# Order of the block products and of the transposes in the first MLP matrices of a two-layer decoder trunk

## The chip, the cores and the metric

The kernel runs on one core of a Trainium2 chip. Its time is the device time of one execution in microseconds. Five engines take part, each with its own queue that is worked off in order: TensorE (PE, with its weight loads PEld), VectorE (DVE), ScalarE (ACT), GpSimd (POOL) and SyncE (SP). SP and POOL only start DMAs here. Engines wait for each other through semaphores.

## The reference

Two decoder layers over 256 tokens of width 2048 in float32. Layer 0 mixes by two recurrent groups, layer 1 by dilated attention; behind each mixer stands an MLP with 8192 hidden features, and a norm closes the whole:

```
def squared_relu_mlp(h, w1, w2):
    return jnp.square(jax.nn.relu(h @ w1)) @ w2

for layer in range(DEPTH):
    hn = rms_norm(h, norm_mix[layer])
    ...
    h = h + mix
    h = h + squared_relu_mlp(rms_norm(h, norm_mlp[layer]), mlp_w1[layer], mlp_w2[layer])
return rms_norm(h, final_norm)
```

The change touches the products with `w1` and, in a detail, with `w2`.

## The kernel before, in words

**Weights.** All weights come from memory in units of 128 partitions x 2048 float32, 1 MB each, in a fixed list (`units`). A unit is loaded by SP into a `raw` tile (three buffers), and then split into two parts: ScalarE copies it into `hi` (line 102), VectorE subtracts and leaves `lo` (line 103); both have three buffers, too. So a unit's split can start once the unit three places before it has been multiplied, and its load once the raw tile three places before it has been split. A product in full precision takes three matmuls for each block of 128 features: x-high with `hi`, x-high with `lo`, x-low with `hi`, in this order (`times`). `unit()` hands out the next unit and fetches ahead, about three units.

**The MLP.** `mlp` goes through the hidden features in four quarters of 2048. For each quarter, `first` is called twice (for `w1`, n = 0 and 2, each gives 1024 of the quarter's features) and then `second` twice (for `w2`, each adds to 1024 of the output columns). Each of these four calls is one run of `blocks`: eight 1 MB blocks of weights, and 180 matmuls of 512 columns. Half of the contraction is done by a scheme of the Strassen kind, with seven block products of 12 matmuls instead of eight; the other half is plain.

The seven products and their operands, by name: a and d multiply plain weight blocks (units 0 and 1); t1, t2, t3 and t4 multiply sums of weight blocks, c multiplies block 5. VectorE makes the sums at line 130: s = a + t1 when a is fetched, s += c when the unit ahead of t2 is fetched. Two sums are made by DMAs that POOL starts and that add in place: t1 += block 5 (line 142, at the same fetch), and, for `w1` alone, s += block 1 (line 148, at the fetch of c), which t4 needs. `t1` and `s` have one buffer each. The plain half consists of four units called n (n6, n7, n2, n3), each with 24 matmuls: 12 for each half of the tokens.

**The banks.** `blocks` holds four accumulators: alpha, delta and gamma of one pool, beta of another that alternates between two banks from block to block. a, t2, t3 and t4 go to beta, t1 and c to alpha, d to gamma. n6 and n7 add to delta and then alpha, n2 and n3 to gamma and then beta. Between products the results that are needed by themselves are read out: in `first`, after a, t1 and t2 by a ScalarE copy (`hold`, line 716), after t3 by VectorE (`u3`, lines 729 and 730), after the last plain product of a sum by `final` (line 742). ScalarE then applies the squared ReLU (lines 720 and 721).

**The transposes.** What a block leaves is put in a list `later` as a function: `to_h` (eight transposes on TensorE, then copies at lines 696 and 697 and the forms for the next matrices at lines 593 to 600) after `first`, and `to_features` (transposes, then lines 235 and 236) after a projection and, in layer 0's last quarter, after `second`. `flush` runs what was in the list at a given moment. In `blocks`, `due` is taken before each n, and the flush stands after its 24 matmuls.

**What sets the order.** TensorE's matmuls and transposes are chained in the order of the program (`mm`, `turn`). The other engines' queues are ordered when the program is built, by a scheduler with priorities (`stream` and `urgent`). The order of the units within a block is written out by hand at the end of the file: `ORDERS[0]` for `w1`, `ORDERS[1]` for `w2`. `plan2` uses it for the list of units, `blocks` for the products.

```
_A = (("a", 0), ("t1", 4))
_B = (("t2", 5), ("c", None))
_C = (("t3", None), ("d", 1), ("n", 2), ("t4", None), ("n", 3))
ORDERS = (_A + (("n", 6),) + _B + (("n", 7),) + _C, _A + (("n", 7),) + _B + (("n", 6),) + _C)
```

Of the kernel before, what the change touches and what calls it, by code (L numbers as in the profile page):

```python
# [41 lines left out]
def trunk_kernel(ctx, tc, x, xtok, cols, tab, masks, pos, fin, w_in, w_gate, w_out, w_qkv, w_o, w1, w2, out):  # L42
# [28 lines left out]
    def plan2(src, i):  # L71
        for what, u in ORDERS[src is w2]:
            units.append((src, None if u is None else i + u, what, i))
# [3 lines left out]
    for step in ORDER.split():  # L77
        src, first, n = where[step[0]]
# [29 lines left out]
    def fetch():  # L108
        u = at[0]
        if u >= len(units):  # L110
            return
        at[0] += 1
        src, i = units[u][:2]
        with stream():
            if len(units[u]) > 2:
                combine(u, *units[u])
                return
            r = wraw.tile([P, 2048], F32, name="raw")
            nc.sync.dma_start(r, src[i])
            made[u] = Weights(r, 1024)  # L120
# [49 lines left out]
    def unit(src, i):  # L170
        u = at[1]
        assert units[u][0] is src and units[u][1] in (None, i), (u, i)
        at[1] += 1
        if u + 2 >= at[0]:
            fetch()
        return made.pop(u)
# [3 lines left out]
    def mm(*args, **kw):  # L180
        chain[:] = [after(T.matmul(*args, **kw), chain)]  # L181
# [4 lines left out]
    later = []  # L186

    def flush(due=None):
        todo = later[:due]
        del later[:due]  # L190
        for f in todo:
            f()
# [455 lines left out]
    def blocks(src, i0, n0, mov, forms, events, final):  # L648
        plain = lambda j, k: (mov[:, k, j * P:j * P + P], mov[:, k, S + j * P:S + j * P + P])
        form = lambda f, k: (forms[:, k, 0, f * P:f * P + P], forms[:, k, 1, f * P:f * P + P])  # L650
        side = {"a": lambda i: plain(0, 2 * i), "d": lambda i: plain(0, 2 * i + 1), "t4": lambda i: plain(1, 2 * i + 1),
                "t1": lambda i: form(3, i), "t2": lambda i: form(0, i), "t3": lambda i: form(1, i),
                "c": lambda i: form(2, i)}
        alpha, delta, gamma = (pmm.tile([P, 512], F32, name="p") for _ in range(3))
        beta = psc.tile([P, 512], F32, name="po" if n0 else "pd", bufs=1)
        bank = {"a": beta, "t1": alpha, "t2": beta, "c": alpha, "t3": beta, "d": gamma, "t4": beta}
        sums = {(0, 0): gamma, (0, 1): beta, (1, 0): alpha, (1, 1): delta}
        opened = []

        def times(bank, w, get):  # L660
            for i in range(4):
                h, l = w.part(i * 512, 512)
                xh, xl = get(i)
                mm(bank, xh, h, start=not any(b is bank for b in opened), stop=False, skip_group_check=True)
                opened.append(bank)
                mm(bank, xh, l, start=False, stop=False, skip_group_check=True)
                mm(bank, xl, h, start=False, stop=i == 3, skip_group_check=True)

        plains = [0, 0]
        for what, u in ORDERS[src is w2]:  # L670
            w = unit(src, None if u is None else i0 + 4 * n0 + u)
            if what != "n":
                times(bank[what], w, side[what])
                if what in events:
                    events[what](bank[what])
                continue
            n, g = divmod(u, 4)
            plains[n] += 1
            due = len(later)
            for j in (1, 0) if n else (0, 1):  # L680
                times(sums[n, j], w, lambda i, j=j, g=g: plain(j, 4 * g + i))
                if plains[n] == 2:
                    final(n, j, sums[n, j])
            flush(due)
# [24 lines left out]
    def first(i0, n0):  # L709
# [23 lines left out]
        def final(n, j, bank):  # L733
            with urgent():
# [5 lines left out]
                else:  # L740
                    y = keep["y2" if n else "y1"]
                    V.tensor_tensor(y, bank, y, OP.subtract if n else OP.add)
                    relu2(n, j, y, y)

        blocks(w1, i0, n0, bufa, formx, {"a": hold("y1", 2), "t1": hold("y4"), "t2": hold("y2"), "t3": u3}, final)

    def second(i0, n0, nrm, r2, r2n, done, gains):
        def to_x(bank, j, n, r, last):
            at = slice(n * 512, n * 512 + 512)
            with urgent():  # L750
                V.scalar_tensor_tensor(xres[:, j, at], bank, r[:, j:j + 1], xres[:, j, at], op0=OP.mult, op1=OP.add)  # L751
                if nrm and last:
                    nrm.add(j, n)

        def u2(bank):
            to_x(bank, 0, n0 + 1, r2n, False)
            if gains:
                gains()

        def u3(bank):  # L760
            to_x(bank, 1, n0 + 1, r2n, True)
            done(n0 + 1)

        blocks(w2, i0, n0, bufb, formh,
               {"a": lambda b: to_x(b, 0, n0, r2, False), "t1": lambda b: to_x(b, 1, n0 + 1, r2, False),
                "t2": u2, "t3": u3},
               lambda n, j, b: to_x(b, j, n0 + n, r2, (n, j) != (1, 1)))
        done(n0)
# [186 lines left out]
WARM = 12  # L955
LINE = 64
SCRATCH = 4096
_A = (("a", 0), ("t1", 4))
_B = (("t2", 5), ("c", None))
_C = (("t3", None), ("d", 1), ("n", 2), ("t4", None), ("n", 3))  # L960
ORDERS = (_A + (("n", 6),) + _B + (("n", 7),) + _C, _A + (("n", 7),) + _B + (("n", 6),) + _C)
T4_DMA = lambda w1, w2: (w1,)
NOSYNC = mybir.DependencyInfo(mybir.DependencyClass.NoSync, mybir.DependencyReason.DATA)

# [102 lines left out]
```

## Time and profile before

| what | us |
|---|---|
| median of 3 runs | 2178.93 (2178.92 to 2179.68) |
| the profiled execution | 2178.8 |
| its span, first to last instruction | 2177.0 |
| TensorE busy | 2148.7 |
| VectorE busy | 1783.6 |
| ScalarE busy | 1261.1 |

The page gives busy time and waits over one execution; lines are those of the kernel before. The two MLPs run from about 426 to 1107 us and from about 1490 us to the end. In the timeline a row gives start, duration, engine, line, operation, output and inputs, and in brackets the idle time before it with what ended it. A row that begins with SPq or POOL is a DMA's start on that queue, not its transfer; the view of the DMA issues gives the time from issue to landing. Matmuls overlap: each is shown with 0.39 us, and they follow each other at a shorter distance, which is read from their starts.

```profile
DMA  8444445577777677787655554556768777777873
...
q1 hardware_dynamic: 58176, 410.89, 53.2%
q0 software_dynamic: 7264, 51.42, 12.8%
...
L103 DVE TENSOR_TENSOR lo<-raw,hi 128x1024 fp32r<-128x1024 f32 (+2 forms) x486 | 822.3, 1709 | 237.7 <-ACT hi L102 219.3
```

The first row is the mean busy share of the 16 DMA engines in 40 slices, in tenths. q1 holds the loads that SP starts, q0 the adding loads that POOL starts, each with its packets, MB and share of the DMA engines' time. The last row is the group of VectorE's splits.

### The profile page before, as it was taken

To read this page: it belongs to the slowest core of one execution; us is meant where nothing else is said; L and a number is where in the kernel's file an instruction comes from. 1 tells how busy PE (TensorE), PEld (TensorE's weight loads), DVE (VectorE), ACT (ScalarE), POOL (GpSimd) and SP (SyncE) were. 2 spreads that over 40 slices of the span, in tenths; PEclk is the share of its full clock that TensorE was granted. 3 is DMA by queue.
4 is the path that set the end of the run, shared out by engine and by line. 5 is a ranking of instruction groups with operands and counts; after the bars stand their busy time and mean duration, and the time that the engine had idled before them with its cause. 6 is when DMAs were issued, how large, how long until landed. Compare 5 with 4: busy or idle time off the path is not lost.

```text
span 2177.0 us, 27718 instructions
## 1 busy us (share of the span) xinstructions
PE 2148.7 (99%) x11044; PEld 1834.7 (84%) x11044; DVE 1783.6 (82%) x2078; ACT 1261.1 (58%) x1429; POOL 44.6 (2%) x57
## 2 busy tenths in 40 slices
PE   9999999999999999999999999999999999999997
PEld 8999998878888888888788888888888888888886
DVE  7776787779879889888877778667898898898897
ACT  7444485566466566466554544455655755755664
POOL 0000000000000000000000000000000000000000
PEclk9999999999999999999999999999999999999999
DMA  8444445577777677787655554556768777777873
GB/s 317 155 157 170 149 156 207 189 235 240 228 236 248 226 247 232 232 251 231 201 207 169 179 175 163 185 193 213 232 221 258 237 224 238 251 231 224 260 238 129
DMA packets 65857, 464.68 MB, mean 213 GB/s; under 512 B 7344, under 2 KB 8112, under 8 KB 10304
## 3 DMA queue, kind: packets, MB, share of 16 engines
q1 hardware_dynamic: 58176, 410.89, 53.2%
q0 software_dynamic: 7264, 51.42, 12.8%
q8 instruction: 87, 1.43, 0.3%
q10 hardware_dynamic: 288, 0.61, 0.1%
q14 instruction: 42, 0.34, 0.0%
HBM read 460.78 MB, written 2.10 MB: 213 GB/s over the span
## 4 chain that ended last, share of the span: by engine, by line
PE 89%; ACT 5%; DVE 3%; issue 2%; DMA 1%; SPq 0%; DVEq 0%; ACTq 0%
PE p L181 63%; PE po L181 11%; PE pd L181 10%; ACT hi L102 3%; PE pl L184 2%; DVE lo L103 1%; PE pl L476 1%; DMA raw<-in_w 0%; ACT y L720 0%; ACT formh L593 0%; ACT y L716 0%; ACT y L721 0%; PE pl L864 0%; DMA xall<-in_x 0%; PE po L885 0%
## 5 line engine op out<-in xcount | busy, mean ns | idle before, releaser
L102 ACT CAST hi<-raw 128x1024 fp32r<-128x1024 f32 (+2 forms) x486 | 689.2, 1443 | 571.4 <-PE p L181 403.1
L103 DVE TENSOR_TENSOR lo<-raw,hi 128x1024 fp32r<-128x1024 f32 (+2 forms) x486 | 822.3, 1709 | 237.7 <-ACT hi L102 219.3
L181 PE MATMUL p<-hi,bufb 128*128 128x512 f32 x1408 | 448.5, 390 | 2.2 <-DVE xall L751 2.1
L181 PE MATMUL p<-hi,bufa 128*128 128x512 f32 x1280 | 412.5, 392 | 11.3 <-ACT y L716 7.9
L181 PE MATMUL p<-bufa,hi 128*128 128x256 f32 (+1 forms) x1792 | 364.9, 317 | 0.1
L181 PEld LDWEIGHTS p<-hi,bufb 128*128 128x128 f32 x1408 | 264.3, 188 | 60.0 <-DVE xall L751 5.6
L181 PEld LDWEIGHTS p<-bufa,hi 128*128 128x128 f32 x1792 | 294.5, 190 | 18.9 <-DVE hz L418 0.3
L181 PEld LDWEIGHTS p<-hi,bufa 128*128 128x128 f32 x1280 | 240.4, 188 | 65.5 <-ACT y L716 11.3
L181 PE MATMUL p<-lo,bufb 128*128 128x512 f32 x704 | 274.1, 389 | 1.0 <-DVE lo L103 1.0
L181 PE MATMUL p<-bufa,lo 128*128 128x256 f32 x1152 | 255.5, 287 | 0.0
L181 PE MATMUL p<-lo,bufa 128*128 128x512 f32 x640 | 250.5, 391 | 1.9 <-DVE lo L103 1.9
L103 DVE TENSOR_TENSOR lo<-s,hi 128x2048 fp32r<-128x2048 f32 x96 | 219.5, 2287 | 23.2 <-ACT hi L102 21.3
L102 ACT CAST hi<-s 128x2048 fp32r<-128x2048 f32 x96 | 183.7, 1913 | 48.1 <-PE po L181 21.7
L181 PEld LDWEIGHTS p<-bufa,lo 128*128 128x128 f32 x1152 | 189.3, 191 | 2.7
L181 PEld LDWEIGHTS p<-lo,bufb 128*128 128x128 f32 x704 | 132.2, 188 | 28.3 <-DVE lo L103 1.4
L181 PEld LDWEIGHTS p<-lo,bufa 128*128 128x128 f32 x640 | 120.4, 188 | 27.1 <-DVE lo L103 3.2
L130 DVE TENSOR_TENSOR s<-s,raw 128x2048 f32<-128x2048 f32 x48 | 109.6, 2284 | 1.7 <-DMA raw<-in_w 1.7
L181 PE MATMUL pd<-hi,bufa 128*128 128x512 f32 x256 | 84.8, 392 | 0.0
L181 PE MATMUL po<-hi,bufa 128*128 128x512 f32 x256 | 84.8, 392 | 0.0
L181 PE MATMUL p<-hi,formx 128*128 128x512 f32 x256 | 84.0, 389 | 0.0
L181 PE MATMUL p<-hi,formh 128*128 128x512 f32 x256 | 84.0, 389 | 0.0
L103 DVE TENSOR_TENSOR lo<-t,hi 128x2048 fp32r<-128x2048 f32 x32 | 73.2, 2287 | 12.4 <-ACT hi L102 12.4
(281 smaller groups left out, 2765.7 us busy)
## 6 DMA issues: line engine op xcount, KB each, us to landing
raw<-in_w SPq DMA_DIRECT2D x224, 1024.0 KB, 5.1
raw<-in_w_qkv SPq DMA_DIRECT2D x48, 1024.0 KB, 4.9
raw<-in_w_in SPq DMA_DIRECT2D x46, 1024.0 KB, 4.9
t<-in_w SPq DMA_DIRECT2D x32, 1024.0 KB, 5.4
t<-in_w POOLq DMA_DIRECT2D x32, 1024.0 KB, 8.8
raw<-in_w_out SPq DMA_DIRECT2D x16, 1024.0 KB, 4.9
s<-in_w POOLq DMA_DIRECT2D x16, 1024.0 KB, 8.9
raw<-in_w_o SPq DMA_DIRECT2D x16, 1024.0 KB, 4.9
```

The lines of the kernel that those rows point to most:

```text
L102: A.copy(h, w)
L103: V.tensor_tensor(l, w, h.bitcast(F32), OP.subtract)
L130: V.tensor_tensor(held[to], held[x], held[y], OP.add)
L181: chain[:] = [after(T.matmul(*args, **kw), chain)]
L184: chain[:] = [after(T.transpose(out_, in_, ident), chain)]
L476: T.matmul(pl[:, j], kq[:, js], halves(qp[:, js], c, True), start=True, stop=True)
```

## The change

In the order for `w1`, d moves from the eighth place to the third, ahead of the first plain product. The order for `w2` stays as it is. And the pending transposes are run at fixed steps of a block, after the product in the third place and after the one in the tenth, in both orders: for `w1` after d (before: after n6) and after t4 (before: after n2), for `w2` after n7 (as before) and after t4 (before: after n2). What is pending is still taken ahead of that product.

```
-        for what, u in ORDERS[src is w2]:
+        for step, (what, u) in enumerate(ORDERS[src is w2]):
             w = unit(src, None if u is None else i0 + 4 * n0 + u)
+            due = len(later) if step in FLUSH[src is w2] else 0
             if what != "n":
                 times(bank[what], w, side[what])
                 if what in events:
                     events[what](bank[what])
+                flush(due)
                 continue
             n, g = divmod(u, 4)
             plains[n] += 1
-            due = len(later)
...
-_A = (("a", 0), ("t1", 4))
-_B = (("t2", 5), ("c", None))
-_C = (("t3", None), ("d", 1), ("n", 2), ("t4", None), ("n", 3))
-ORDERS = (_A + (("n", 6),) + _B + (("n", 7),) + _C, _A + (("n", 7),) + _B + (("n", 6),) + _C)
+ORDERS = ((("a", 0), ("t1", 4), ("d", 1), ("n", 6), ("t2", 5), ("c", None), ("n", 7), ("t3", None), ("n", 2),
+           ("t4", None), ("n", 3)),
+          (("a", 0), ("t1", 4), ("n", 7), ("t2", 5), ("c", None), ("n", 6), ("t3", None), ("d", 1), ("n", 2),
+           ("t4", None), ("n", 3)))
+FLUSH = ((2, 9), (2, 9))
```

Since the list of units follows the same table, SP loads d's block in the third place, too. The lines of the new kernel from 672 on are those of the old one plus one.

## Prediction

> **What bounds the kernel now.** First the page's totals, then TensorE's list of waits, then the timeline of each engine at the seams between blocks.
>
> ```profile
> span 2177.0 us, 27718 instructions
> PE 2148.7 (99%) x11044; PEld 1834.7 (84%) x11044; DVE 1783.6 (82%) x2078; ACT 1261.1 (58%) x1429; POOL 44.6 (2%) x57
> ...
> PEclk9999999999999999999999999999999999999999
> ...
> PE p L181 <- ACT y L716: 7.9, 8, 1.0
> ...
> PE p L181 <- DVE bufa L236: 2.7, 2, 1.4
> ```
>
> TensorE is busy nearly throughout, so a new order can only remove waits or make some. Eight times it waits for ScalarE's copy at L716. That is the second block of each pair of `first` blocks: n6's second half writes alpha, and the copy of t1's result out of alpha is not done. Twice it waits for the features of L236, at the start of each MLP. What such waits cost, and the pace without them:
>
> ```profile
> 478.14 0.39 PE L181 MATMUL p<-hi,bufa 128*128 128x512 f32 x1
> 479.52 0.50 PE L181 MATMUL p<-hi,bufa 128*128 128x512 f32 x1 [0.99 <-ACT y L716]
> 479.86 0.40 PE L181 MATMUL p<-lo,bufa 128*128 128x512 f32 x1
> ...
> 444.06 0.39 PE L181 MATMUL p<-lo,bufa 128*128 128x512 f32 x1
> 445.81 0.72 PE L181 MATMUL p<-hi,bufa 128*128 128x512 f32 x2 [1.36 <-DVE bufa L236]
> 446.37 0.40 PE L181 MATMUL p<-lo,bufa 128*128 128x512 f32 x1
> ...
> 482.38 1.03 PE L184 MATMUL pl<-tab__181,y 128*128 128x128 f32 x8
> 558.67 5.44 PE p L181 x24
> ```
>
> A matmul takes 5.44/24 = 0.227 us. From 478.14 to 479.86 there should have been 0.45 us and there were 1.72: 1.27 lost. From 444.06 to 446.37 there should have been 0.68 and there were 2.31: 1.63 lost. The eight transposes of a flush take 1.0.
>
> **The change part by part.** No matmul, split or DMA is added; units change places, and with them the loads on SP's queue, since each unit fetches its own block.
>
> *What goes.* Between t1 and n6 now stand the 12 matmuls of d, 2.72 us, more than the 0.99 us by which the copy was late: 8 x 1.27 = 10.2 us go. The pending transposes run after d, one product earlier, and n6 follows them before n7 needs the features: 2.72 + 2.72 = 5.44 us more room against a wait of 1.36, so 2 x 1.63 = 3.3 us go.
>
> *What comes.* `raw` has three buffers. Raw loads of a block went a, n6, c, n7, d; now they go a, d, n6, c, n7. A load waits until the buffer three places before it has been split. c's load waited for n3 of the block before; now it stands where n7's stood and waits for the split of a. Here is that seam before a `first` block that follows a `second` block:
>
> ```profile
> 587.66 2.29 DVE L130 TENSOR_TENSOR s<-raw,t 128x2048 f32<-128x2048 f32 x1
> 588.94 1.92 ACT L102 CAST hi<-raw 128x2048 fp32r<-128x2048 f32 x1 [3.52 <-PE po L181]
> 590.48 0.87 POOL L142 DMA_DIRECT2D t<-in_w  x1 [40.26 <-DVE s L130]
> 590.89 2.29 DVE L103 TENSOR_TENSOR lo<-raw,hi 128x2048 fp32r<-128x2048 f32 x1 [0.94 <-ACT hi L102]
> ...
> 587.77 0.33 SPq L127 DMA_DIRECT2D raw<-in_w  x1
> 593.21 0.33 SPq L127 DMA_DIRECT2D raw<-in_w  x1
> ...
> raw<-in_w SPq DMA_DIRECT2D x1, 1024.0 KB, 4.8
> raw<-in_w SPq DMA_DIRECT2D x1, 1024.0 KB, 7.5
> raw<-in_w SPq DMA_DIRECT2D x1, 1024.0 KB, 8.0
> ...
> 596.53 2.28 DVE L130 TENSOR_TENSOR s<-s,raw 128x2048 f32<-128x2048 f32 x1
> 596.90 0.39 PE L181 MATMUL pd<-hi,bufa 128*128 128x512 f32 x1
> ```
>
> The block starts at 596.90. a's split (ACT from 588.94, DVE 590.89 to 593.18) lets the load of 593.21 go. The load of 587.77, c today, took 4.8 us; the one of 593.21, n7 today, took 7.5, because the accumulating load of t1 (POOL, 590.48) shares the DMA engines. Nobody was hurt: n7 is needed late. Now c stands there and lands at 593.21 + 7.5 = 600.7. The same load at the other five such seams took up to 8.0 (at 761.61, the last of these rows); I take 7.7, so c lands 4.0 us after the block's start.
>
> VectorE takes its work in order, and in the built order of the changed kernel the addition s += c (L130) still stands ahead of the split of the third unit, now d:
>
> ```
> s += c (L130)    lo of d (L103)    lo of n6 (L103)    lo of t2 (L103)
> ```
>
> So d, which does not need c at all, waits behind it. That such a chain reaches TensorE is seen once already:
>
> ```profile
> 1052.24 0.87 POOL L142 DMA_DIRECT2D t<-in_w  x1 [38.62 <-DVE s L130]
> ...
> 1053.80 9.58 DMA raw<-in_w
> ...
> 1057.23 0.87 DVE L236 SCALAR_TENSOR_TENSOR bufa<-pl,c__83,bufa 128x256 fp32r<-128x256 f32 x2
> ...
> 1063.47 2.29 DVE L130 TENSOR_TENSOR s<-s,raw 128x2048 f32<-128x2048 f32 x1 [1.09 <-DMA raw<-in_w]
> 1066.34 2.28 DVE L103 TENSOR_TENSOR lo<-raw,hi 128x2048 fp32r<-128x2048 f32 x1
> 1068.68 0.50 PE L181 MATMUL p<-lo,bufb 128*128 128x512 f32 x1 [0.96 <-DVE lo L103]
> ```
>
> The addition starts 0.09 us after the landing, and TensorE restarts 0.06 after the split's end. Dependent VectorE work of this size follows at 2.20 us. So from c's landing to d's first `lo` matmul: 0.09 + 2.20 + 2.29 + 0.06 = 4.64.
>
> *Seam after a `second` block, six times* (quarters 1 to 3, two layers). TensorE reaches that matmul 25 x 0.227 = 5.67 us after the block's start; it gets it at 4.0 + 4.6 = 8.6. With 0.1 for the slow restart (479.52 to 479.86 against 0.227) that is 3.1 us, 6 x 3.1 = 18.6. The splits of n6 and t2 then come in time (they end 2.2 and 4.4 us after d's; d and n6 take 2.72 and 5.44).
>
> *Seam between two `first` blocks, eight times.* Times from the start of the second block. The last units of the first block end at -17.3 (n7), -14.6 (t3), -9.2 (n2), -6.4 (t4), then transposes (1.0) and n3 (5.4). The split of t4 gets its buffer at n7's end and is done 4.4 later (from 588.94 to 593.18 for a's split, with 0.2 before it), at -12.9; behind it stand L730, which is L729 today (0.7, below), and the addition s = a + t1 (2.2), to -10.0. t1's accumulating load starts 0.6 later (590.48 against 587.66 + 2.29): A = -9.4. After L731 (0.7) n3's split ends at -7.1 and lets n6's load go (A + 2.3); a's split ends 4.4 after n2, at -4.8, and lets c's go (A + 4.6), behind n6's in the same queue. The nearest such pair:
>
> ```profile
> 604.84 0.86 POOL L148 DMA_DIRECT2D s<-in_w  x1 [13.50 <-DVE lo L103]
> ...
> 607.29 0.33 SPq L127 DMA_DIRECT2D raw<-in_w  x1
> 612.25 0.33 SPq L127 DMA_DIRECT2D raw<-in_w  x1
> ...
> raw<-in_w SPq DMA_DIRECT2D x1, 1024.0 KB, 8.1
> raw<-in_w SPq DMA_DIRECT2D x1, 1024.0 KB, 6.9
> ...
> 475.13 0.42 DVE L600 TENSOR_TENSOR y<-pl,y 128x256 f32<-128x256 f32 x1
> 498.54 0.68 DVE L729 TENSOR_TENSOR y<-y,po 128x512 f32<-128x512 f32 x1
> ```
>
> The first load, 2.45 after the accumulating one, landed 10.5 after it; the second at 14.3 (issued later than c's would be). The lower bound is a lone load, 4.8 after issue: A + 9.6. I take A + 13.5, near the pair since the queue is the same: 4.1 after the block's start. L600 (0.4) stands between the addition and d's split here, so TensorE gets d's `lo` at 4.1 + 4.64 + 0.4 = 9.1: 3.5 late, 3.6 with the restart. Bounds: no wait (c at 0.2) and 4.3 (c at 4.9). Less the 1.27 already counted as gone: 8 x 3.6 = 28.8 against -10.2.
>
> *Small ones.* t3's result is read from beta by L730 before n2's second half writes there: the room shrinks from 24 matmuls (5.44 us) to 12 (2.72). By the walk above L730 ends at -12.2 and the writes start at -14.6 + 2.7 = -11.9: no wait, 0.3 us spare; below that it costs what is missing, 0 to 0.5 each. Gamma is needed earlier by d, two products after its last reader: free. In `second` the order of products stays; later transposes put two L236 (1057.23: 0.87 for two) ahead of the split that ended at 1068.6: +0.8, once.
>
> The sum on the profiled execution, 2178.8 us (span 2177.0 and 1.8 around it; the median shown is 2178.93, 0.1 more): 2178.8 - 10.2 - 3.3 + 18.6 + 28.8 + 0.8 = 2213.5. I say 2213.
>
> [...]
>
> **The rivals.** (1) *Only the old waits go*, the faster side: 2178.8 - 10.2 - 3.3 = 2165.3. It needs c on the spot by 5.67 - 4.64 = 1.0 us after the block's start, a load under 4.7 us at the first seam. For it: lone loads take 4.8. Against: the six loads of 7.5 to 8.0. 5%. (2) *The first seam stalls, the second does not*, since c lands there as a lone load would: 2213.5 - 28.8 = 2184.7. For it: no row shows just this pair with c's early issue. Against: n6's load ahead in the same queue. 10%. (3) *The waits make TensorE slow as well.* If the 12 matmuls of d after each of 14 waits took double, 14 x 2.72 = 38 us more: 2251. Against it: after the longest wait, 1.36, the granted clock stays at 9 tenths or more in every slice (the PEclk row); but 3 us is beyond any row here. 4%. [...] (4) *Also L730 late*, or the seam into `second` (c there waits for n3's split, which ends later too): 14 x 0.5 = 7 more, 2220; within my range.
>
> **How the numbers follow.** My own case, with (4), has 81%: from 2204 (c 0.6 earlier at the second seam, 7.5 at the first) to 2225 (c at 4.9, L730 late). To leave out no more than 2 in 10 the range reaches down toward rival 2: 2196 to 2229. Within 0.2%, 4.4 us, counts as no change, about what a measurement here can tell. Slower: 81 + 10 + 4 = 95%, less 3 for a mix of 1 and 2 that ends level: 92%; same 3%; faster 5%.
>
> **What would show it.** TensorE's waits: the entry for L716 and the one for L236 gone, a new one for L103, some 14 times near 2.9 to 3.4 us, each at d's first `lo` matmul, and VectorE idle before L130 for the raw load. Wrong: s += c with no wait for a DMA, or TensorE's waits at another product, or c's load under 7 us at the seam after `second`.

## The result, and the profile after

The changed kernel takes 2230.41 us, the median of five runs (2228.75 to 2231.23), against 2178.93 for the kernel before in as many (2178.82 to 2179.68): ratio 1.0233, 95% interval 1.0218 to 1.0248. It is slower by 51.5 us. The prediction said 2213, 2196 to 2229; the sign and the place are right, the size is too small by 17 us. The profiled execution is one of 2230.41 with a span of 2228.6.

First the page of the changed kernel, then TensorE's and VectorE's lists of waits (what waits, for whom, us in total, times, longest); the last row is that of the kernel before.

```profile
span 2228.6 us, 27714 instructions
PE 2169.7 (97%) x11044; PEld 1847.2 (83%) x11044; DVE 1783.0 (80%) x2078; ACT 1262.8 (57%) x1429; POOL 44.6 (2%) x57
...
PEclk9999999999999999999999999999999999999999
```

```profile
PE p L181 <- DVE lo L103: 44.6, 18, 3.9
...
DVE s L130 <- DMA raw<-in_w: 52.7, 23, 3.7
...
DVE s L130 <- DMA raw<-in_w: 1.7, 3, 1.1
```

TensorE's entries for the copy (now L717) and for L236 are gone, as the prediction wanted. In their place stands one entry for VectorE's `lo`, 18 waits with 44.6 us in all; 14 of them, 40.9 us, are at d. VectorE in turn waits 52.7 us for raw loads ahead of L130, where before it waited 1.7. And TensorE is busy 21 us longer with the same 11044 matmuls: something made them slower. The row of the granted clock doesn't show it, since a slice of 56 us averages it away; the mean over the span does, 0.989 against 0.999.

The seam after a `second` block, in the timeline of each engine. The block starts at 598.19:

```profile
591.76 0.85 POOL L142 DMA_DIRECT2D t<-in_w  x1 [40.26 <-DVE s L130]
...
592.18 2.29 DVE L103 TENSOR_TENSOR lo<-raw,hi 128x2048 fp32r<-128x2048 f32 x1 [0.95 <-ACT hi L102]
...
594.50 0.33 SPq L127 DMA_DIRECT2D raw<-in_w  x1
...
raw<-in_w SPq DMA_DIRECT2D x1, 1024.0 KB, 7.4
...
598.19 0.39 PE L181 MATMUL pd<-hi,bufa 128*128 128x512 f32 x1
...
602.03 2.29 DVE L130 TENSOR_TENSOR s<-s,raw 128x2048 f32<-128x2048 f32 x1 [2.89 <-DMA raw<-in_w]
604.24 4.49 DVE L103 TENSOR_TENSOR lo<-raw,hi 128x2048 fp32r<-128x2048 f32 x2
...
606.58 0.50 PE L181 MATMUL p<-lo,bufa 128*128 128x512 f32 x1 [2.56 <-DVE lo L103]
```

This is the chain that was forecast. a's split ends at 594.47, c's load goes at 594.50 and takes 7.4 us beside the accumulating load, s += c starts 0.1 us after its landing, d's `lo` comes behind it, and TensorE goes on 8.4 us after the block's start. The same at a seam between two `first` blocks, where n6's load and c's are the two starts of the first row, and the block starts at 468.41:

```profile
461.25 2.92 SPq L127 DMA_DIRECT2D raw<-in_w  x2
...
471.75 2.29 DVE L130 TENSOR_TENSOR s<-s,raw 128x2048 f32<-128x2048 f32 x1 [2.17 <-DMA raw<-in_w]
473.96 0.42 DVE L600 TENSOR_TENSOR y<-pl,y 128x256 f32<-128x256 f32 x1
474.29 2.28 DVE L103 TENSOR_TENSOR lo<-raw,hi 128x2048 fp32r<-128x2048 f32 x1
```

What wasn't in the sum is seen on TensorE behind the wait, at the second seam of the first kind:

```profile
778.00 0.39 PE L181 MATMUL p<-hi,bufa 128*128 128x512 f32 x1
781.08 0.78 PE L181 MATMUL p<-lo,bufa 128*128 128x512 f32 x1 [2.69 <-DVE lo L103]
781.65 1.05 PE L181 MATMUL p<-hi,bufa 128*128 128x512 f32 x2
782.51 0.63 PE L181 MATMUL p<-lo,bufa 128*128 128x512 f32 x1
...
784.84 0.39 PE L181 MATMUL p<-lo,bufa 128*128 128x512 f32 x1
785.06 0.62 PE L181 MATMUL p<-hi,bufa 128*128 128x512 f32 x2
```

And the table by stretches (from and to, length, then busy time of each engine; the granted clock is the third number from the end):

```profile
781.08:782.08 1.00, 1.00 (x3) 0.81 (x3) 1.00 (x1) 0.00 (x0) 0.00 (x0) 0.53 0.07 8
782.08:783.08 1.00, 1.00 (x4) 0.81 (x3) 1.00 (x1) 0.00 (x0) 0.00 (x0) 0.50 0.89 147
783.08:784.08 1.00, 1.00 (x4) 0.81 (x3) 1.00 (x2) 0.00 (x0) 0.00 (x0) 0.50 0.97 410
784.08:785.08 1.00, 1.00 (x5) 0.76 (x5) 1.00 (x1) 0.00 (x0) 0.00 (x0) 0.77 0.99 418
...
652.54:653.54 1.00, 1.00 (x4) 0.86 (x5) 1.00 (x2) 1.00 (x2) 0.00 (x0) 1.00 0.12 25
```

From 781.08 to 784.84 there are nine matmuls, 3.76 us where 9 x 0.227 = 2.04 were due: 1.7 us lost while the clock is at half. After the wait that ends at 652.54 (2.36 us) the clock stays full. Of the 14 waits at d, 11 are followed by such a stretch (all six after `second`, five of eight between `first` blocks), and so is the one wait of `second` in layer 0's last quarter (1.93 us).

The difference of the spans, 51.6 us, by blocks (from a block's first matmul to the next one's, before and after):

| blocks | before | after | together | predicted |
|---|---|---|---|---|
| first of an MLP, 2 | 44.24 to 44.27 | 42.60 | -3.3 | -3.3 |
| `first` after `second`, 6 | 41.69 to 41.71 | 46.16 to 46.50 | +27.6 | +18.6 |
| `first` after `first`, 8 | 43.88 to 43.90 | 45.26 to 48.46 | +24.8 | +28.8 - 10.2 |
| `second` with the lone wait | 427.67 (with layer 1's mixer) | 429.23 | +1.6 | +0.8 |
| all others | | | +1.0 | 0 |

### The profile page after: what moved, and what is told of

It is laid out like the page before. It is cut to its first block, busy times and chain, and to the rows that moved or that the text cites. A ratio compares the mean times of both kernels' runs of the same rounds, so it can differ in the third digit from the quotient of the medians.

```text
span 2228.6 us, 27714 instructions
## 1 busy us (share of the span) xinstructions
PE 2169.7 (97%) x11044; PEld 1847.2 (83%) x11044; DVE 1783.0 (80%) x2078; ACT 1262.8 (57%) x1429; POOL 44.6 (2%) x57
## 4 chain that ended last, share of the span: by engine, by line
PE 85%; DVE 6%; DMA 4%; issue 3%; ACT 2%; SPq 0%; DVEq 0%; ACTq 0%
PE p L181 63%; PE po L181 11%; PE pd L181 7%; DVE lo L103 4%; DMA raw<-in_w 4%; ACT hi L102 2%; PE pl L184 1%; PE pl L476 1%; DMA raw<-in_w_in 0%; PE pl L865 0%; PE po L886 0%; DVE y L731 0%; DVE y L730 0%; PE pd L878 0%; DVE xall L752 0%
## 5 line engine op out<-in xcount | busy, mean ns | idle before, releaser
L181 PE MATMUL p<-hi,bufa 128*128 128x512 f32 x1280 | 426.6, 404 | 0.9 <-ACT hi L102 0.9
L181 PE MATMUL p<-lo,bufa 128*128 128x512 f32 x640 | 259.5, 405 | 42.5 <-DVE lo L103 42.5
L181 PEld LDWEIGHTS p<-hi,bufa 128*128 128x128 f32 x1280 | 248.6, 194 | 52.8 <-ACT hi L102 1.3
L130 DVE TENSOR_TENSOR s<-s,raw 128x2048 f32<-128x2048 f32 x48 | 109.8, 2288 | 52.7 <-DMA raw<-in_w 52.7
L181 PE MATMUL pd<-hi,bufb 128*128 128x512 f32 x256 | 82.7, 389 | 0.0
```

What stands on the lines that cost most here:

```text
L130: V.tensor_tensor(held[to], held[x], held[y], OP.add)
```

## The experiments

The theory after the result: c's load is late, by its place in the list and by the transfer beside it; s += c holds up d's residual on VectorE, where d's `lo` stands behind it (604.24, behind the addition at 602.03); and the waits of 2 to 4 us bring a half clock of 3.41 us, as in the trace of the changed kernel. The rivals: the new place of the transposes is to blame; s += c is harmless, or costs by its own time; the matmuls are slower for a reason that has nothing to do with the wait. In the expectations, d's first residual matmul is the one that reads d's `lo`. The clock given with each time is the mean granted over the profiled execution.

**The new places of the transposes alone**, with the old order of the products:

```
-ORDERS = ((("a", 0), ("t1", 4), ("d", 1), ("n", 6), ("t2", 5), ("c", None), ("n", 7), ("t3", None), ("n", 2),
-           ("t4", None), ("n", 3)),
+ORDERS = ((("a", 0), ("t1", 4), ("n", 6), ("t2", 5), ("c", None), ("n", 7), ("t3", None), ("d", 1), ("n", 2),
+           ("t4", None), ("n", 3)),
```

> The old order of the products with the new places of the transposes. My theory (c's load comes late because d's load stands ahead of it and takes its raw buffer): no wait for c's load, TensorE waits for the copy at the line of hold as before (8 times near 1 us), 2175 to 2183 us, granted clock 0.999. Rival A (the later transposes load VectorE at the seam): at least half of the added 51 us, so over 2200 us.

2184.82 us, ratio 1.0024 (1.0014 to 1.0034), clock 0.998. TensorE's waits:

```profile
PE p L181 <- ACT y L717: 12.0, 8, 1.5
...
PE p L181 <- DVE bufa L236: 2.7, 2, 1.4
```

This is 2 us above what was expected: the old wait for the copy grows from 0.99 to 1.5 us, eight times, 4.1 us in all. None of the 14 waits at d arises. The transposes' places cost at most 6 us by themselves; without the new order the 51 do not arise.

**The new order alone**, with the transposes behind each plain product as before:

```
-            due = len(later) if step in FLUSH[src is w2] else 0
+            due = len(later) if what == "n" else 0
```

> The new order of the products, with transposes after each plain product as before. My theory: the 14 waits at d's first lo matmul stay, and with them the half clock; 2222 to 2238 us, clock near 0.989. Rival A (the transposes): back to 2175 to 2190 us.

2271.28 us, ratio 1.0424 (1.0409 to 1.0440), clock 0.986: 33 us above the top of the forecast.

```profile
PE pl L184 <- ACT y L722: 47.2, 16, 3.3
PE p L181 <- DVE lo L103: 22.3, 12, 3.1
```

The waits at d after `second` stay (2.8 to 3.1). Between two `first` blocks they fall to 0.9 us or less, so the expectation that all 14 stay is missed for eight of them. There TensorE is held at the end of the block before, while the loads go on: c's load starts 7.4 to 9.0 us ahead of the block's start, 4.6 in the changed kernel. New are 16 waits of transposes for ScalarE's squared ReLU. By the order in the program, with d gone from between t3 and n2, the results that t3 completes reach the transposes 12 matmuls sooner; no run tests this by itself. So rival A falls, the later transposes do not make the loss, and the new order without them is slower still.

**s += c out of d's way.** In the first matrices the addition stands behind the subtraction of n6's split on VectorE; c's load stays as late as it is:

```
-            add("s", "s", "c")
+            if src is w2:
+                add("s", "s", "c")
+        if what == "t2" and src is w1:
+            after(add("s", "s", "c"), split_last)
```

> The changed kernel, but in the first MLP matrices VectorE adds c to s behind the split of n6 instead of ahead of the split of d. c's load is as late as in the changed kernel. My theory: d waits for nothing, TensorE's waits at d go, the clock stays at 0.999; with the old waits gone too, 2163 to 2172 us. Rival B (two short units in a row leave the split of d too little time whatever stands ahead of it): waits of more than 1 us stay at d, over 2190 us.

2189.58 us, ratio 1.0049 (1.0033 to 1.0066), clock 0.999: 41 us of the loss are gone, and the slow stretches with them. It isn't the 2163 to 2172 that was expected, because the lateness moves on:

```profile
PE po L186 <- DVE lo L103: 5.8, 8, 0.8
PE p L186 <- DVE lo L103: 4.9, 7, 2.1
PE pl L189 <- ACT y L727: 4.5, 7, 0.8
```

t2, which does need s, now waits up to 0.8 us, and transposes wait for ScalarE. The link from s += c to d is shown: the edit moves the addition alone, c's load starts as late as before and takes 8.0 us at the first seam after `second`, and no wait at d is left. So rival B falls.

**Work in place of the wait.** 12 extra matmuls into a bank that nobody reads, ahead of d in the 14 blocks; later 5 of them. Their results are not used:

```
+            if what == "d" and src is w1 and (n0 or i0 % 64):
+                fill = psc.tile([P, 512], F32, name="pt", bufs=1)
+                for _ in range(12):
+                    mm(fill, mov[:, 0, :P], mov[:, 0], start=True, stop=True)
```

> The changed kernel with 12 extra matmuls (2.7 us, results not used) ahead of d in the 14 blocks that wait there. If the half clock comes from TensorE's idle time: the extra matmuls fill the wait, the clock stays at 0.997 or more, the wait is paid but not the slow matmuls (12 times about 1.7 us), 2205 to 2214 us. Rival C (the matmuls after the wait are slow for another reason, such as the loads that run then): no gain, 2228 to 2240 us, clock near 0.989.

> Edit: 5 extra matmuls of 128x512 into a bank nobody reads ahead of d's product in the 14 blocks where the wait arises, where the earlier filler run had 12; their results are not used. 5 matmuls take about 1.1 us, so the idle stretch left in each block is about 1.3 to 2.8 us where the changed kernel has 2.4 to 3.9. If an idle stretch has to be longer than about 2 us for the granted clock to halve afterwards, half of the blocks keep the full clock, and the time is 2215 to 2225. If any idle stretch above 1 us can do it, most blocks still have the slow stretch and the time is 2226 to 2234. If the clock only depends on stretches above 3.4 us, none has it and the time is 2205 to 2212.

With 12 (2.72 us): 2218.17 us, ratio 1.0178 (1.0163 to 1.0193), clock 0.998. With 5 (1.14 us): 2207.74 us, ratio 1.0130 (1.0110 to 1.0150), clock 0.998. Both do more work than the changed kernel and take less time. With 5, at the seam that the profile after showed, timeline and then the table by stretches:

```profile
774.86 1.30 PE L181 MATMUL pt<-bufa 128*128 128x512 f32 x5
776.00 0.39 PE L181 MATMUL p<-hi,bufa 128*128 128x512 f32 x1
777.94 0.50 PE L181 MATMUL p<-lo,bufa 128*128 128x512 f32 x1 [1.55 <-DVE lo L103]
```

```profile
777.94:778.94 1.00, 1.00 (x4) 0.86 (x5) 1.00 (x1) 0.00 (x0) 0.00 (x0) 1.00 0.23 41
```

The wait is shorter by what was filled in, and the clock stays full. The six blocks after `second` take 44.5 to 44.8 us instead of 46.2 to 46.5, 1.7 less, just what the nine slow matmuls lost. So the slow clock makes about 20.4 us (12 stretches of 1.7) of the 22.7 between the two kernels (2230.4 - 2207.7), and it hangs on the wait, not on the matmuls: rival C falls. The figure of 2207.7 lies in the band that was written for a limit of 3.4 us of idle time; no run shows such a limit, and the changed kernel itself has half clock after 1.93 and 2.39 us. All that the run says is that idle times of 1.2 to 1.9 us, and here one of 2.5, left the clock alone. The run with 12 is slower than that with 5, and 4 us above its band: in four of the 14 blocks a wait of 0.6 to 1.3 us remains behind the whole filler, and four `second` blocks have a new wait of 0.8 to 1.5 us for `lo`. Why the weights are later there was not followed.

**c's load right behind d's**, so that c gets the third raw buffer and n6 the one that a frees:

```
+            if what == "d" and src is w1:
+                load("c", i0 + 5)
...
-            load("c", i0 + 5)
+            if src is w2:
+                load("c", i0 + 5)
```

> Edit: in the first MLP matrices c's raw load is issued right behind d's instead of behind n6's, so that c takes the third raw buffer and n6 takes the one that a's split frees. All else as in the changed kernel. Theory (c's load waits for a's split because it is the fourth load over three buffers, so s += c is late and holds back d's residual on the in-order VectorE): c lands some 4 us or more earlier, the 14 waits of 2.4 to 3.9 us at d's first residual matmul go or fall below 0.5 us each, the granted clock is back at 0.998 or more, and the time is 2163 to 2180. Rival D (the load in the late place is what matters, whichever it is): n6's load is now the late one and its own split stalls TensorE at n6's first matmul by 1 us or more in most of the 14 blocks; time 2190 to 2215. Rival E (s += c itself, 2.29 us of VectorE time ahead of d's subtract, is the cost and not its wait for the load): the waits at d stay above 1.5 us and the time stays above 2205.

2180.89 us, ratio 1.0008 (0.9999 to 1.0018), clock 0.997. It is 0.9 us above the band, and its mechanism holds: of the 14 waits 11 are gone and three of 1.2 us are left, none of them after `second`. TensorE's waits:

```profile
PE p L184 <- DVE lo L103: 7.3, 7, 1.9
PE p L184 <- ACT y L720: 3.2, 8, 0.8
```

The wait of 1.9 us in the first row is the lone one of `second`, and the one half stretch of this run from the first MLP to the end follows it. n6 does not wait for its weights, and s += c, with the same 2.29 us in the same place, does no harm when c is there. Both rivals fall.

**The accumulating load later, by its place in the program.** It is written one step further on, at the fetch of c's split:

```
-            nc.gpsimd.dma_start(held["t1"], src[i0 + 5], accum_op=OP.add)
+            if src is w2:
+                nc.gpsimd.dma_start(held["t1"], src[i0 + 5], accum_op=OP.add)
...
         if what == "c" and src in T4_DMA(w1, w2):
+            nc.gpsimd.dma_start(held["t1"], src[i0 + 5], accum_op=OP.add)
```

> Edit: in the first MLP matrices the accumulating load of t1 is issued when c's own split is fetched, later than in the changed kernel by one product, so that it does not move while c's load moves. c's load keeps its late place. Theory with the shared DMA as the larger half (1 MB in 7.5 to 8.0 us beside the accumulating load, 4.8 us alone): c lands some 2.7 us earlier, the waits at d's first residual matmul fall from 2.4 to 3.9 us to 0.8 us or less, granted clock 0.998 or more, time 2168 to 2185. Rival F (the late issue of c's load alone makes the wait, the sharing adds little): the waits stay above 2 us in the 14 blocks and the time stays within 2222 to 2234. If the accumulating load then comes too late for t3, a new wait stands at t3's first residual matmul and the time is up to 15 us above the first figure.

2231.19 us, ratio 1.0237 (1.0221 to 1.0252), clock 0.987. This would speak for the rival, but the edit did not do what it was for. GpSimd's queue and SP's in the timeline:

```profile
591.61 0.85 POOL L149 DMA_DIRECT2D t<-in_w  x1 [40.26 <-DVE s L130]
...
594.35 0.33 SPq L127 DMA_DIRECT2D raw<-in_w  x1
```

The accumulating load still starts as soon as t1 has been read, 2.74 us ahead of c's, as in the changed kernel (591.76 and 594.50): nothing else stands in its queue to hold it. The run decides nothing.

**The accumulating load later, in fact.** A copy of one column of s on GpSimd, behind s += c, stands ahead of it; c's load stays in its late place:

```
-            nc.gpsimd.dma_start(held["t1"], src[i0 + 5], accum_op=OP.add)
             add("s", "s", "c")
+            if src is w1:
+                i = nc.gpsimd.tensor_copy(late, held["s"][:, :1])
+                after(nc.gpsimd.dma_start(held["t1"], src[i0 + 5], accum_op=OP.add), [getattr(i, "ins", i).name])
```

> Edit: as the changed kernel, c's load in its late place, but in the first MLP matrices a one-column GpSimd copy that reads s behind s += c stands ahead of the accumulating load of t1 on the GpSimd queue, so that this load is issued only when c has landed and been added (some 12 us later than now). Theory (half of c's lateness is the transfer it shares with the accumulating load): c's 1 MB lands in about 4.9 us instead of 7.4, s += c starts 2.5 us earlier, the 14 waits at d's first residual matmul fall from 2.4 to 3.9 us to 0 to 1.3 us, no slow clock follows (mean granted clock 0.997 or more), and the time is 2172 to 2192. Rival F (the sharing does not matter, the late issue does it alone): c still takes above 6.5 us, the waits stay above 2 us, and the time stays at 2222 to 2234. If the accumulating load is then too late for t3, a new wait of 1 us or more stands at t3's first residual matmul.

2191.51 us, ratio 1.0052 (1.0037 to 1.0068), clock 0.998, within the band. The seam after `second`, in which the block starts at 595.3; the time from c's start to its landing stands in the third row:

```profile
600.97 0.85 POOL L148 DMA_DIRECT2D t<-in_w  x1
...
591.62 0.33 SPq L128 DMA_DIRECT2D raw<-in_w  x1
...
raw<-in_w SPq DMA_DIRECT2D x1, 1024.0 KB, 4.8
...
596.50 2.29 DVE L131 TENSOR_TENSOR s<-s,raw 128x2048 f32<-128x2048 f32 x1 [0.23 <-DMA raw<-in_w]
598.71 4.49 DVE L103 TENSOR_TENSOR lo<-raw,hi 128x2048 fp32r<-128x2048 f32 x2
```

```profile
PE p L186 <- DVE lo L103: 9.5, 11, 2.0
PE pd L186 <- DVE y L735: 7.5, 6, 1.6
```

Alone, c's load takes 4.8 us instead of 7.4, and the wait at d in these blocks is gone, although the load starts as late as ever. So after `second` the late place and the shared transfer are both needed for the loss: taking away either removes it. Rival F falls. Between two `first` blocks most of it goes; three waits at d of 1.1 to 1.6 us stay, in the blocks in which c's load takes 6.0 to 6.3 us although the accumulating load has not been issued. What slows it there was not followed. New is a wait of 1.1 to 1.6 us, six times, for the subtraction at L735 (L729 before the change).

**Two tries for a faster kernel.** Both have c's load behind d's. The first gives the transposes out one step later, `FLUSH = ((3, 9), (2, 9))`:

> Edit: the kernel with c's load right behind d's, and in the first MLP matrices the pending transposes are given out one step later (behind n6's product instead of behind d's). It is a try for a version faster than both: eight blocks there still wait 0.3 to 0.8 us for ScalarE's copy of a result bank, which stands behind a split and the copies of transposes. If the copies of the transposes ahead of it are the cause, these waits go and the time is 2170 to 2178. If the split ahead of it is, nothing changes, 2178 to 2184. If the transposes then come too late for the block that needs them, 2184 to 2200.

2245.01 us, ratio 1.0300 (1.0286 to 1.0314), clock 0.992, far outside all three bands:

```profile
PE pl L187 <- ACT y L725: 24.7, 8, 3.1
```

The copies of the transposes no longer stand ahead of ScalarE's copy of t1's result, and TensorE's waits for that copy stay all the same (eight, 0.6 us). The transposes of the tenth step now wait 3.1 us for the squared ReLU, and L236 is late again. Why the built order of ScalarE turns out so much worse for one step was not followed further.

The second has c's load behind d's and the accumulating load behind s += c:

> Edit: both, c's load right behind d's and the accumulating load of t1 issued only when c has been added. If the three remaining waits of 1.2 us at d's first residual matmul come from c's load sharing with the accumulating load, they go and the time is 2172 to 2179; if not, it stays at 2179 to 2184; if t3 then waits for the accumulating load, it is above 2184.

2176.49 us, ratio 0.9986 (0.9978 to 0.9995), clock 0.998: within the first band and faster than both kernels, by 0.14% than the one before.

```profile
PE p L188 <- ACT y L724: 5.4, 8, 0.7
PE p L188 <- DVE lo L103: 4.0, 4, 2.1
```

No wait at d is left in any of the 14 blocks. The waits of the second row are in `second` blocks. But the eight blocks between `first` and `first` take 43.6 us, where 43.88 were taken before and 42.6 would be without the old wait: the copy (L724 here) is late by 0.7 us again.

## Why the prediction was right or wrong

*What goes.* Both old waits go, as said, and in the first blocks the 3.3 us come out to the tenth. The 10.2 us go, too, though the time does not show it: the three blocks between `first` and `first` that kept the full clock are 45.3 to 45.5 us long, 1.5 above before, which is their wait of 2.4 to 2.6 with its restart less the 1.27. But in the last run, with c in time, only 0.3 us of the 1.27 stays gone. ScalarE's copy there starts 12.0 us after the block's start, behind the split of c and the copies of the features; in the kernel before it started at 8.7, in the changed kernel, ahead of that split, at 9.2. "More than the 0.99 us by which the copy was late" counted the room that TensorE gives and not what ScalarE has ahead of the copy.

*The late load of c.* Right in each step: the place behind a's split, 7.4 us for the load (7.7 taken), s += c ahead of d's split, TensorE going on 4.7 us after the landing (601.90 to 606.58; 4.64 taken). The run with the addition moved, the one with c's load moved and the one with the other load moved each cut one link, and each took the wait at d away after `second`; the last two leave three of eight between `first` blocks.

*The seam after `second`.* At 778.00 to 781.08, 2.85 us are lost ahead of the matmul (3.08 less 0.227), where 3.0 and 0.1 for the restart were forecast. The remaining 1.7 of the 4.6 us per block were not in the sum.

*The seam between two `first` blocks.* The waits shown are 2.36 to 3.94 us, 3.08 on average, with 0.16 more lost as above 3.2 where 3.5 were taken. c landed 3.3 us after the block's start at the shown seam, instead of 4.1, and up to 4.9 at others. The bounds (0 and 4.3) held.

*The small ones.* L730 made no wait, as said. The lone wait of `second` cost 1.6 instead of 0.8, a half clock again.

*The step that failed* is the dismissal of rival 3, "the waits make TensorE slow as well", which got 4% and whose price stayed out of the sum and of the range. Its mechanism is what happened, 12 times: 1.7 us each, 20.4 us, where the rival had priced 2.72 for each of 14. Without these the table's sum is 51.6 - 20.4 = 31.2 us, against 34.7 forecast; with them the time lies 1.4 us above the range. The ground given was that the clock held after the longest wait of before, 1.36 us, and the same sentence said that 3 us was beyond any row. The PEclk row could not have carried it in any case: its slices are 54 us long, and it reads the same after the change, with 12 half stretches in it. An unknown cost without a row at its size has to be in the range, not in a tail of 4%. In the changed kernel half clock came after waits of 1.93 and 2.39 us, and 1.7 us are lost in each half stretch of 3.41 us.

## What to carry to other kernels

Moving a product in a hand-written order moves its load in the queue, and with a few buffers the load that falls on the late place is another one than that which was moved: write down, for each load, which buffer it gets and what stands in order behind its consumer. A wait of TensorE is to be priced with a slow stretch behind it, here 1.7 us: by the table below as likely as not from 1.8 to 2.7 us (17 of 33), nearly always above that (34 of 37). A transfer's time is to be taken from a row where the same neighbours are in flight: here 4.8 us alone and 7.4 beside an accumulating load.

## What the runs showed of the hardware

In these runs the half clock has no sharp limit in the length of a wait. Over the profiles of before, after and all ten experiments, TensorE's waits of 1.4 us and more from the MLP of layer 0 to the end, by the length shown and by whether the clock fell to half within the next 6 us:

| wait, us | clock stays full | half clock |
|---|---|---|
| 1.4 to 1.8 | 18 | 0 |
| 1.8 to 2.3 | 5 | 6 |
| 2.3 to 2.7 | 11 | 11 |
| 2.7 to 3.2 | 2 | 19 |
| 3.2 to 3.8 | 1 | 14 |
| over 3.8 | 0 | 1 |

The shortest with half clock has 1.83 us, the longest without has 3.75, twice as much. The wait of 3.75 us is in the run with the accumulating load moved in the program only (from and to, length, busy time of each engine; the granted clock is the third number from the end):

```profile
1565.38:1568.79 3.41, 1.49 (x7) 0.91 (x5) 3.04 (x3) 3.01 (x4) 0.00 (x0) 1.00 0.00 0
1568.79:1572.20 3.41, 1.58 (x7) 1.31 (x8) 3.41 (x3) 2.62 (x3) 0.00 (x0) 1.00 0.16 34
```

TensorE is idle for 3.75 of these 6.82 us, and the clock stays at 1.00. Waits of the same length ended both ways, too: the run with the transposes given out one step later has two of 1.83 us, which end at 1054.44 and at 2153.60. The 3 us behind each:

```profile
1054.44:1055.44 1.00, 1.00 (x4) 0.86 (x5) 1.00 (x2) 1.00 (x1) 0.00 (x0) 1.00 0.31 41
1055.44:1056.44 1.00, 1.00 (x6) 0.80 (x5) 1.00 (x1) 0.75 (x1) 0.00 (x0) 1.00 0.86 131
1056.44:1057.44 1.00, 0.79 (x4) 0.33 (x2) 1.00 (x2) 0.00 (x0) 0.00 (x0) 1.00 0.96 401
...
2153.60:2154.60 1.00, 1.00 (x4) 0.85 (x5) 1.00 (x2) 1.00 (x1) 0.00 (x0) 1.00 0.14 33
2154.60:2155.60 1.00, 1.00 (x5) 0.78 (x5) 1.00 (x1) 0.75 (x1) 0.00 (x0) 0.77 0.93 147
2155.60:2156.60 1.00, 1.00 (x4) 0.81 (x3) 1.00 (x2) 0.00 (x0) 0.00 (x0) 0.50 1.00 418
```

What else decides is not shown here.
